# Two matmuls instead of three for the transposed products: both activation parts side by side as one 512-wide moving operand

## The chip, the cores and the metric

One NeuronCore of a Trainium2 chip. The metric is the device time of one execution in microseconds. The engines that matter here: PE (matrix multiply, with its weight load PEld), DVE (VectorE), ACT (ScalarE), SP (issues the DMAs). PE multiplies a stationary operand of 128x128 by a moving operand (here of 128 to 512 columns) and writes fp32 sums into PSUM, from which DVE and ACT read them. The program's PSUM pools hold eight banks of 512 fp32 columns: four for the products' sums, four for everything else.

## The reference

A stack of three layers on 256 tokens of 2048 features, all in fp32. What matters is that nearly all work is products of the activations with large weights:

```python
proj = jnp.einsum("bsd,de->bse", x, w_in) + b_in            # layer 1: conv branch, windowed attention
h = x @ w_in                                                 # layer 2: indexer-selected attention
q, g = _split(x @ w_q, (ATTN_W_2, ATTN_W_2))                 # layer 3: stick-breaking attention
x = _layer_norm(DN_ALPHA * x + y, ln_g[i], ln_b[i])          # after each
x = x + (p[i] @ w_ple[i]) * jax.nn.sigmoid(x @ w_ple_gate[i])
```

## The kernel before

Every product is made in a reduced-precision fp32 type (fp32r) from exact parts: an operand is rounded to a high part and the rest is its low part. A product is then three matmuls: high x high, high x low, low x high. Weights stream from DRAM in granules of 128 x 1024 (512 KB): a granule is loaded by SP (L247), rounded by ACT (`whi`, L265), and the rest is taken by DVE (`wlo`, L266). `whi` and `wlo` have four buffers each, and the code fetches two granules ahead of the one in use. The activations (`Act`) lie transposed, [feature, token], in tiles of four K tiles (K tile: 128 features), high and low parts in tiles of their own.

Two routines make the products, both a loop over the 16 K tiles of a chunk of weight columns. `gemm` has the activations stationary and up to 512 weight columns moving; it gives [token, column]. `gemm_T` has 128 weight columns stationary and 256 tokens moving; it gives [column, token], and makes three matmuls of 128x256 per K tile and 128 columns (L325 high x high, L326 high x low, L327 low weights x high). A chunk of `gemm_T` is 512 columns, in two PSUM tiles of one bank; the pool `acc` has four banks.

After a chunk its sums are read out of PSUM directly: by ACT with bias and function (`projected`, L468, in layer 1; `silu_chunk`, L964), by DVE and ACT in `glu` (L493), by DVE's rotation (`rope_T`, L839 and L840, for `Turned`), and by `Split` (L987 ACT high part, L988 DVE low part, L991 ACT copy). Between granules `side.pump()` hands out steps of other work (the convolution L481, attention, norms) to all engines. Each engine runs its instructions in the order that the tile scheduler fixed when the program was built.

Of the kernel before, what the change touches and what calls it, by code (L numbers as in the profile page):

```python
# [45 lines left out]
# Per weight: the chunks in the order of use, each as (column ranges, K tiles).  # L46
# [3 lines left out]
def _pairs(base, j):  # L50
    """Heads i and 8 + i side by side, for i of the j-th four."""
    return tuple(r for i in range(4 * j, 4 * j + 4) for r in ((base + 64 * i, 64), (base + 512 + 64 * i, 64)))
# [3 lines left out]
    **{f"vg{c}": ((CV + 256 * c, 256), (CG + 256 * c, 256)) for c in range(4)},  # L56
    "kv": _c(KK, 256),
    "q0": _pairs(QQ, 0),
    "ag0": _pairs(AG, 0),
    "q1": _pairs(QQ, 1),  # L60
    "ag1": _pairs(AG, 1),
    "cg0": _c(CT, 512),
    "cg1": _c(CT + 512, 512),
}
CHUNKS_1 = {key: (ranges, ALL) for key, ranges in CHUNKS_1.items()}
# The last columns of a row of the residual in smaller chunks.
# [10 lines left out]
    "k": (_c(2048, 512), ALL),  # L77
    "v": (_c(2560, 512), ALL),
    **{f"{n}{c}": (_c(o + 512 * c, 512), ALL) for c in range(4) for n, o in (("q", 0), ("g", 3072))},
# [3 lines left out]
CHUNKS_KV = {f"{n}{c}": (_c(o + 512 * c, 512), ALL) for c in range(4) for n, o in (("k", 0), ("v", 2048))}  # L83
CHUNKS_QB = {f"{n}{c}": (_c(o + 512 * c, 512), ALL) for c in range(4) for n, o in (("q", 0), ("g", 2048))}
# [15 lines left out]
def _plan():  # L100
    """The chunks in the order of their products."""
    w2 = [("w_in_a_2", key) for key in CHUNKS_2]
    w3 = [(w, f"{n}{c}") for c in range(4) for w, n in (("w_kv_b_2", "k"), ("w_q_b_2", "q"), ("w_kv_b_2", "v"), ("w_q_b_2", "g"))]
# [13 lines left out]
def _group(ranges, kts):  # L117
    """K tiles loaded at a time: about 4 KB a partition, less at the start."""
    if ranges == CHUNKS_1["vg0"][0]:
        return 1  # L120
# [3 lines left out]
def _column_tiles(chunks):  # L124
    """Per chunk, the number of its first tile of 128 columns."""
# [15 lines left out]
class Side:  # L141
    """Work beside the stream of weights, given out in small steps from each of some lanes."""
# [30 lines left out]
def tile_net(ctx: ExitStack, tc: tile.TileContext, t: dict, out: bass.AP):  # L173
# [10 lines left out]
    acc = ctx.enter_context(tc.tile_pool(name="acc", bufs=4, space=bass.MemoryType.PSUM))  # L184
# [29 lines left out]
    # additive mask [q, keys]: own block causal | previous block s > q, own block causal  # L214
# [25 lines left out]
    def load(stream, key, g):  # L240
        """The chunk's weights for a group of K tiles, on their way from DRAM."""
# [14 lines left out]
    def fetch(p, keep=False):  # L256
        """A group of weights as two exact parts."""
# [10 lines left out]
    def prefetch(*wanted):  # L268
        """The first groups of some chunks ahead of their turn, in steps."""
# [9 lines left out]
    def granules(stream, key, events):  # L279
        """The chunk's weights as they come: K tile, its first and last flags, both parts."""  # L280
# [35 lines left out]
    def gemm_T(stream, key, act, events=None):  # L316
        """[column, token] per two tiles of 128 columns."""
        nf = _cols(STREAMS[stream][key][0]) // P
        ps = [acc.tile([P, 2, S], F32, tag="acc", name=uid("acc")) for _ in range(nf // 2)]
        for kt, first, last, wh, wl in granules(stream, key, events):  # L320
            ah, al = act(kt, slice(0, S))
            for f in range(nf):
                o = ps[f // 2][:, f % 2, :]
                fs = slice(f * P, (f + 1) * P)
                nc.tensor.matmul(o, wh[:, fs], ah, start=first and f % 2 == 0, stop=False)  # L325
                nc.tensor.matmul(o, wh[:, fs], al, start=False, stop=False)  # L326
                nc.tensor.matmul(o, wl[:, fs], ah, start=False, stop=last and f % 2 == 1)  # L327
        return ps

    class Act:  # L330
        """Activations transposed, [feature, token], as two exact parts."""

        def __init__(self, kts=ALL):
            quarters = sorted({kt // 4 for kt in kts})
            self.hi = {q: unit((P, 4, S), F32R) for q in quarters}
            self.lo = {q: unit((P, 4, S), F32R) for q in quarters}

        def __call__(self, kt, s):
            q, k = divmod(kt, 4)
            return self.hi[q][:, k, s], self.lo[q][:, k, s]  # L340

        def parts(self, kt, n):
            q, k = divmod(kt, 4)
            return self.hi[q][:, k:k + n, :], self.lo[q][:, k:k + n, :]
# [6 lines left out]
    def transposes(blocks):  # L351
        """[token, 128] blocks -> a bank of them transposed, side by side."""
# [5 lines left out]
    def transpose_into(act, kt, nat, f0, n=2):  # L358
        """n K tiles from features f0.. of nat [token, token tile, feature]."""
# [4 lines left out]
    def turn_T(dst, nat, blocks):  # L364
        """128 features at a time of nat [token, token tile, feature] -> dst [feature, block, token]."""
# [31 lines left out]
    class Norm:  # L397
        """Layer norm over the features of z, [token, token tile, 512] per tile."""
# [9 lines left out]
        def apply(self, act):  # L408
            """z to (z - mean) / deviation in place; the operand of the products with scale and shift."""
# [23 lines left out]
        def affine(self):  # L433
            """Scale and shift of z itself, for the residual."""
# [6 lines left out]
    # ================= layer 1 =================  # L441
# [21 lines left out]
    def projected(key, out_, func, skip=0, events=None):  # L463
        """A chunk of the input projection, [column, token], with its bias and func."""
        ps = gemm_T("w_in", key, xact, events)
        for f in range(skip, 2 * len(ps)):
            b = tiles1[key] + f
            nc.scalar.activation(out_[:, f - skip, :], ps[f // 2][:, f % 2, :], func, bias=bias1[:, b:b + 1])  # L468
        return ps
# [14 lines left out]
    def glu(c):  # L484
        sg = short((P, 2, S))
        events = {kt: (lambda kt=kt: load_x(kt)) for kt in range(0, KT, 2)} if c == 0 else None
        if c == 0:
            load = events[14]
            events[14] = lambda: (load(), load_params())
        ps = projected(f"vg{c}", sg, AF.Sigmoid, 2, events)  # L490
        for f in range(2):
            ct, b = 2 * c + f, tiles1[f"vg{c}"] + f
            nc.vector.scalar_tensor_tensor(  # L493
                hT[ct // 4][:, ct % 4, :], ps[0][:, f, :], bias1[:, b:b + 1], sg[:, f, :], ALU.add, ALU.mult
            )
            side.add(conv(ct), CONV_RATE[ct % 2], "conv")
# [3 lines left out]
    def soften(heads, mask, scale):  # L500
        """Transposed probabilities [key, query] of some heads, in steps; the last value is a list."""
# [55 lines left out]
    def weigh(o, v, p):  # L557
        """o [feature, query] = values under the transposed probabilities of both blocks of keys."""
# [570 lines left out]
```

## Time and profile before

| | |
|---|---|
| three runs | 1467.13, 1467.75, 1468.92 us; median 1467.75 |
| the profiled execution | span from first to last instruction 1465.3 us |
| PE busy | 1453.9 us (99%), 10092 matmuls |
| PEld busy | 1353.8 us (92%) |
| DVE busy | 1000.1 us (68%) |
| ACT busy | 768.0 us (52%) |
| three lines of `gemm_T` | 6048 of the 10092 matmuls |

A group's row reads: line, engine, operation, out<-in by the program's names, shape, count | busy us, mean ns of one | idle time before it and what ended it. Matmuls are pipelined: the duration of one is longer than the distance from its start to the next one's, and the distance is what a stream of them costs.

### The profile page before, as it was taken

Reading aid. Unit: us, or ns where it says so; the run is one execution under the profiler, and the core shown is the slowest. Engines: PE = TensorE matmul, PEld = TensorE weight load, DVE = VectorE, ACT = ScalarE, POOL = GpSimd, SP = SyncE. Lnnn points to the kernel's source line nnn. Section 1 sums busy time; section 2 is a strip of 40 time slices with the busy share of each in tenths; the row PEclk is TensorE's granted clock in tenths of the full one; section 3 lists DMA queues with packets and bytes.
Section 4 is the critical chain, followed back from the end, with each engine's and each line's share of the span. In section 5 each row is a group of like instructions: output and inputs, shape, how many; then the busy total and the mean of one; then the engine's idle time right before and its main releaser. Section 6 shows DMA issues by size and latency. Waiting matters only on the chain.

```text
span 1465.3 us, 25141 instructions
## 1 busy us (share of the span) xinstructions
PE 1453.9 (99%) x10092; PEld 1353.8 (92%) x10092; DVE 1000.1 (68%) x1529; ACT 768.0 (52%) x1133; POOL 24.2 (2%) x51
## 2 busy tenths in 40 slices
PE   8999999999999999999999999999999999999998
PEld 8999999888997999999898899899999998989888
DVE  6998888898679857756758664545555556475854
ACT  6345777465544456546544444644655646554442
POOL 0000000000000000000000000100100001000000
PEclk9999999999999999999999999999999999999999
DMA  9855544556384655455765666555556565587472
GB/s 308 275 186 173 158 159 145 185 185 225 98 249 150 201 151 166 148 172 157 260 195 152 183 176 185 163 170 187 162 171 176 169 175 170 172 266 218 129 221 81
DMA packets 79813, 266.27 MB, mean 182 GB/s; under 512 B 9408, under 2 KB 10048, under 8 KB 79696
## 3 DMA queue, kind: packets, MB, share of 16 engines
q1 hardware_dynamic: 79632, 264.63, 58.8%
q8 instruction: 79, 1.29, 0.4%
q14 instruction: 38, 0.31, 0.1%
q0 software_dynamic: 64, 0.03, 0.0%
HBM read 262.53 MB, written 2.10 MB: 181 GB/s over the span
## 4 chain that ended last, share of the span: by engine, by line
PE 97%; DVE 1%; DMA 0%; issue 0%; ACT 0%; DVEq 0%
PE acc L325 17%; PE acc L326 16%; PE acc L327 16%; PE acc L311 14%; PE acc L312 14%; PE acc L313 14%; PE pt L355 1%; PE o L568 1%; PE pT L544 1%; PE o L569 0%; PE z L1024 0%; PE s L511 0%; PE z L1006 0%; PE o L559 0%; PE s L509 0%; PE z L1010 0%
## 5 line engine op out<-in xcount | busy, mean ns | idle before, releaser
L266 DVE TENSOR_TENSOR wlo<-raw,whi 128x1024 fp32r<-128x1024 f32 (+3 forms) x475 | 564.7, 1190 | 368.9 <-ACT whi L265 367.7
L265 ACT CAST whi<-raw 128x1024 fp32r<-128x1024 f32 (+3 forms) x475 | 485.4, 1024 | 551.7 <-PE acc L326 287.9
L325 PE MATMUL acc<-u,whi 128*128 128x256 f32 x2016 | 576.3, 286 | 5.5 <-ACT whi L265 5.5
L327 PE MATMUL acc<-u,wlo 128*128 128x256 f32 x2016 | 571.5, 283 | 0.0
L326 PE MATMUL acc<-u,whi 128*128 128x256 f32 x2016 | 571.3, 283 | 0.0
L325 PEld LDWEIGHTS acc<-u,whi 128*128 128x128 f32 x2016 | 387.6, 192 | 10.6 <-ACT whi L265 5.5
L326 PEld LDWEIGHTS acc<-u,whi 128*128 128x128 f32 x2016 | 387.8, 192 | 0.0
L327 PEld LDWEIGHTS acc<-u,wlo 128*128 128x128 f32 x2016 | 387.5, 192 | 0.0
L311 PE MATMUL acc<-whi,u 128*128 128x512 f32 (+3 forms) x1004 | 358.7, 357 | 0.0
L313 PE MATMUL acc<-whi,u 128*128 128x512 f32 (+3 forms) x1004 | 356.2, 355 | 0.0
L312 PE MATMUL acc<-wlo,u 128*128 128x512 f32 (+3 forms) x1004 | 355.6, 354 | 0.0
L313 PEld LDWEIGHTS acc<-whi,u 128*128 128x128 f32 x1004 | 189.8, 189 | 25.0 <-DVE u L349 0.2
L311 PEld LDWEIGHTS acc<-whi,u 128*128 128x128 f32 x1004 | 189.8, 189 | 24.8 <-issue 1.3
L312 PEld LDWEIGHTS acc<-wlo,u 128*128 128x128 f32 x1004 | 189.9, 189 | 23.6 <-issue 0.3
L481 DVE SCALAR_TENSOR_TENSOR u<-u,convw,u 128x255 f32<-128x255 f32 (+16 forms) x240 | 110.3, 466 | 4.5
L348 ACT CAST u<-h 128x512 fp32r<-128x512 f32 (+1 forms) x32 | 18.1, 567 | 31.8 <-DVE h L581 24.4
L349 DVE TENSOR_TENSOR u<-h,u 128x512 fp32r<-128x512 f32 (+1 forms) x32 | 19.9, 622 | 16.5 <-ACT u L348 16.5
L438 DVE TENSOR_TENSOR u<-u,h 128x1024 f32<-128x1024 f32 x24 | 28.4, 1220 | 3.3 <-DMA h<-in_ln_g 3.3
L996 POOL TENSOR_SCALAR_AFFINE_SELECT h<-h 128x256 f32<-128x256 f32 x32 | 18.1, 565 | 757.6 <-DVE h L1016 734.8
L524 ACT ACTIVATE u<-u,negm 128x128 f32<-128x128 f32 x64 | 28.4, 445 | 3.9 <-DVE negm L516 3.7
L265 ACT CAST u<-raw 128x1024 fp32r<-128x1024 f32 (+1 forms) x17 | 17.2, 1014 | 14.7 <-DMA raw<-in_w_ple 9.1
L426 ACT ACTIVATE h<-pt,normp 128x256 f32<-128x256 f32 x48 | 22.2, 618 | 0.0
(192 smaller groups left out, 932.0 us busy)
## 6 DMA issues: line engine op xcount, KB each, us to landing
raw<-in_w_in_a SPq DMA_DIRECT2D x80, 512.0 KB, 3.8
raw<-in_w_in SPq DMA_DIRECT2D x76, 512.0 KB, 3.6
raw<-in_w_gate SPq DMA_DIRECT2D x64, 512.0 KB, 4.0
raw<-in_w_kv_b SPq DMA_DIRECT2D x64, 512.0 KB, 3.6
raw<-in_w_q_b SPq DMA_DIRECT2D x64, 512.0 KB, 3.6
raw<-in_w_out SPq DMA_DIRECT2D x32, 512.0 KB, 3.6
raw<-in_w_out_a SPq DMA_DIRECT2D x32, 512.0 KB, 3.9
raw<-in_w_out_b SPq DMA_DIRECT2D x32, 512.0 KB, 4.4
```

Source lines behind the costliest of these rows:

```text
L265: nc.scalar.copy(hi, raw)
L266: return hi, lo, nc.vector.tensor_tensor(lo, raw, hi.bitcast(F32), ALU.subtract)
L311: nc.tensor.matmul(o, ah, wh, start=first, stop=False)
L312: nc.tensor.matmul(o, ah, wl, start=False, stop=False)
L313: nc.tensor.matmul(o, al, wh, start=False, stop=last)
L325: nc.tensor.matmul(o, wh[:, fs], ah, start=first and f % 2 == 0, stop=False)
L326: nc.tensor.matmul(o, wh[:, fs], al, start=False, stop=False)
L327: nc.tensor.matmul(o, wl[:, fs], ah, start=False, stop=last and f % 2 == 1)
L426: nc.scalar.activation(v[:, i, :], pt[:, i * S:(i + 1) * S], AF.Identity, bias=normp[:, self.i, 1, kt + i:kt + i + 1], scale=normp[:, self ...
L438: nc.vector.tensor_tensor(self.z[c], self.z[c], r.unsqueeze(1).broadcast_to([P, 2, 512]), op)
L481: nc.vector.scalar_tensor_tensor(o[:, d:], h[:, :S - d], w, o[:, d:], ALU.mult, ALU.add)
L524: nc.scalar.activation(sc[:, i, cs], sc[:, i, cs], AF.Exp, bias=negm[:, i, tt:tt + 1], scale=-1.0, accum_out=den[:, i, tt:tt + 1],)
```

## The change

`gemm_T` makes two matmuls per K tile and 128 columns. `Act` now holds, for each K tile, the high part and the low part next to each other (256 + 256 columns), and the first matmul has high weights against all 512 of these columns; its sums fill a whole bank, high x high in columns 0 to 255 and high x low in 256 to 511. The second has low weights against the high part and adds to columns 0 to 255. The two halves must be added afterwards: the new `total` copies the second half to SBUF with ACT (with bias or scale) and adds the first half with DVE. Since 128 weight columns now fill a bank, chunks of `gemm_T` are 256 columns (two banks) instead of 512 (two banks); `acc` has two tiles of two banks. `gemm` takes its two banks as one such tile. All readers of `gemm_T`'s sums go by `total`'s result. The first chunk of layer 1 stays at 512 columns. Comments and docstrings were dropped as well.

```diff
-    acc = ctx.enter_context(tc.tile_pool(name="acc", bufs=4, space=bass.MemoryType.PSUM))
+    acc = ctx.enter_context(tc.tile_pool(name="acc", bufs=2, space=bass.MemoryType.PSUM))
...
     def gemm(stream, key, act, events=None):
-        ps = [acc.tile([P, 512], F32, tag="acc", name=uid("acc")) for _ in range(2)]
+        both = acc.tile([P, 2, 512], F32, tag="acc", name=uid("acc"))
+        ps = [both[:, tt, :] for tt in range(2)]
...
     def gemm_T(stream, key, act, events=None):
         nf = _cols(STREAMS[stream][key][0]) // P
-        ps = [acc.tile([P, 2, S], F32, tag="acc", name=uid("acc")) for _ in range(nf // 2)]
+        ps = [acc.tile([P, 2, 2, S], F32, tag="acc", name=uid("acc")) for _ in range(nf // 2)]
         for kt, first, last, wh, wl in granules(stream, key, events):
-            ah, al = act(kt, slice(0, S))
+            both, ah = act.both(kt), act(kt, slice(0, S))[0]
             for f in range(nf):
-                o = ps[f // 2][:, f % 2, :]
+                o = ps[f // 2][:, f % 2]
                 fs = slice(f * P, (f + 1) * P)
-                nc.tensor.matmul(o, wh[:, fs], ah, start=first and f % 2 == 0, stop=False)
-                nc.tensor.matmul(o, wh[:, fs], al, start=False, stop=False)
-                nc.tensor.matmul(o, wl[:, fs], ah, start=False, stop=last and f % 2 == 1)
+                nc.tensor.matmul(o, wh[:, fs], both, start=first, stop=False)
+                nc.tensor.matmul(o[:, 0, :], wl[:, fs], ah, start=False, stop=last)
         return ps
 
+    def total(out_, ps, bias=None, scale=1.0):
+        t = short((P, 2, S))
+        if bias is None:
+            nc.scalar.activation(t, ps[:, :, 1, :], AF.Copy, scale=scale)
+        else:
+            for f in range(2):
+                nc.scalar.activation(t[:, f, :], ps[:, f, 1, :], AF.Identity, bias=bias1[:, bias + f:bias + f + 1])
+        out_ = t if out_ is None else out_
+        if scale == 1.0:
+            nc.vector.tensor_tensor(out_, ps[:, :, 0, :], t, ALU.add)
+        else:
+            nc.vector.scalar_tensor_tensor(out_, ps[:, :, 0, :], scale, t, ALU.mult, ALU.add)
+        return out_
+
     class Act:
         def __init__(self, kts=ALL):
-            quarters = sorted({kt // 4 for kt in kts})
-            self.hi = {q: unit((P, 4, S), F32R) for q in quarters}
-            self.lo = {q: unit((P, 4, S), F32R) for q in quarters}
+            self.pairs = {p: unit((P, 2, 2, S), F32R) for p in sorted({kt // 2 for kt in kts})}
+
+        def both(self, kt):
+            return self.pairs[kt // 2][:, kt % 2].rearrange("p h s -> p (h s)")
...
     def silu_chunk(stream, key, act):
-        ps = gemm_T(stream, key, act)
         sg = unit((P, 4, S))
-        for f in range(2):
-            nc.scalar.activation(sg[:, 2 * f:2 * f + 2, :], ps[f], AF.Silu)
+        for f, h in enumerate("xy"):
+            ps, = gemm_T(stream, f"{key}{h}", act)
+            nc.scalar.activation(sg[:, 2 * f:2 * f + 2, :], total(None, ps), AF.Silu)
...
     class Split:
...
-                nc.scalar.activation(self.hi[:, hs, :], p, AF.Copy, scale=scale)
-                nc.vector.scalar_tensor_tensor(
-                    self.lo[:, hs, :], p, scale, self.hi[:, hs, :].bitcast(F32), ALU.mult, ALU.subtract
-                )
-                nc.scalar.activation(self.late[:, hs, :], p[:, :, P:S], AF.Copy, scale=scale)
+                p, = gemm_T(stream, f"{name}{h}", xact)
+                w = total(None, p, scale=scale)
+                nc.scalar.copy(self.hi[:, hs, :], w)
+                nc.vector.tensor_tensor(self.lo[:, hs, :], w, self.hi[:, hs, :].bitcast(F32), ALU.subtract)
+                nc.scalar.copy(self.late[:, hs, :], w[:, :, P:S])
```

The first rows of PE's order, where layer 1's first chunk begins. `u_103` and `u_107` are the high and low parts of the first K tiles in the kernel before; in the changed one `u_103` holds both. Before:

```order
L325 MATMUL acc_131<-u_103,whi_139 128x256
L326 MATMUL acc_131<-u_107,whi_139 128x256
L325 MATMUL acc_132<-u_103,whi_139 128x256
L327 MATMUL acc_131<-u_103,wlo_140 128x256
L325 MATMUL acc_131<-u_103,whi_139 128x256
L326 MATMUL acc_131<-u_107,whi_139 128x256
L327 MATMUL acc_131<-u_103,wlo_140 128x256
L326 MATMUL acc_132<-u_107,whi_139 128x256
```

and in the changed kernel:

```order
L338 MATMUL acc_130<-u_103,whi_138 128x512
L339 MATMUL acc_130<-u_103,wlo_139 128x256
L338 MATMUL acc_130<-u_103,whi_138 128x512
L339 MATMUL acc_130<-u_103,wlo_139 128x256
L338 MATMUL acc_131<-u_103,whi_138 128x512
L339 MATMUL acc_131<-u_103,wlo_139 128x256
```

Three rows of 256 columns became one of 512 and one of 256, and the first row now needs both parts of the activations.

DVE's order in layer 1 at the end of a chunk of the gated values, among weight granules (`wlo`) and convolution steps. Before:

```order
L266 TENSOR_TENSOR wlo_806<-raw_769,whi_805 128x1024
L493 SCALAR_TENSOR_TENSOR u_116<-acc_477,bias_115,h_476 128x256 x2
L481 SCALAR_TENSOR_TENSOR u_118<-u_116,convw,u_118 128x232
L481 SCALAR_TENSOR_TENSOR u_118<-u_116,convw,u_118 128x254
L481 SCALAR_TENSOR_TENSOR u_118<-u_116,convw,u_118 128x231
```

and in the changed kernel:

```order
L278 TENSOR_TENSOR wlo_678<-raw_649,whi_677 128x1024
L510 SCALAR_TENSOR_TENSOR u_118<-u_116,convw,u_118 128x234
L352 TENSOR_TENSOR h_638<-acc_530,h_638 128x512
L510 SCALAR_TENSOR_TENSOR u_118<-u_116,convw,u_118 128x233
L529 TENSOR_TENSOR u_116<-h_638,h_525 128x512
L510 SCALAR_TENSOR_TENSOR u_118<-u_116,convw,u_118 128x232
L694 SCALAR_TENSOR_TENSOR u_670<-u_670,h_673 128x512
L510 SCALAR_TENSOR_TENSOR u_118<-u_116,convw,u_118 128x231
L694 SCALAR_TENSOR_TENSOR u_670<-u_670,h_673 128x512
```

The two 256-wide gates became one 512-wide sum (L352) and one 512-wide product (L529); the sigmoid's chunk has a sum of its own earlier.

ACT's order in layer 3 at the end of the first key chunk (`Split`). Before:

```order
L265 CAST whi_9993<-raw_9956 128x1024
L987 ACTIVATE u_9982<-acc_9740 128x512
L265 CAST whi_10023<-raw_9997 128x1024
L991 ACTIVATE h_9984<-acc_9740 128x256
L987 ACTIVATE u_9982<-acc_9741 128x512
L265 CAST whi_10053<-raw_10027 128x1024
L991 ACTIVATE h_9984<-acc_9741 128x256
```

and in the changed kernel:

```order
L277 CAST whi_8694<-raw_8676 128x1024
L346 ACTIVATE h_8665<-acc_8576 128x512
L277 CAST whi_8716<-raw_8698 128x1024
L1028 CAST u_8573<-h_8665 128x512
L1030 COPY h_8575<-h_8665 128x256
L277 CAST whi_8738<-raw_8720 128x1024
L277 CAST whi_8770<-raw_8742 128x1024
L277 CAST whi_8792<-raw_8774 128x1024
L346 ACTIVATE h_8760<-acc_8671 128x512
```

Of PSUM ACT now reads only the second half (L346); the high part and the copy come from SBUF, and the second 256 columns follow four granules later instead of at once.

## Rows read from the trace of the kernel before

**Rows 1.** The page: busy time of each engine with its share of the span, and DVE's busy tenths and the granted TensorE clock in 40 slices of the span.

```profile
PE 1453.9 (99%) x10092; PEld 1353.8 (92%) x10092; DVE 1000.1 (68%) x1529; ACT 768.0 (52%) x1133; POOL 24.2 (2%) x51
...
DVE  6998888898679857756758664545555556475854
...
PEclk9999999999999999999999999999999999999999
```

**Rows 2.** All waits of PE in the whole span: engine and line, what it waited for, us in total, times, longest.

```profile
PE acc L325 <- ACT whi L265: 5.5, 1, 5.5
PE ix L889 <- ACT h L892: 0.6, 1, 0.6
PE acc L311 <- DVE u L431: 0.2, 1, 0.2
```

**Rows 3.** Groups by shape: the three matmuls of `gemm_T`, one of their weight loads, and the 512-wide matmul of `gemm`.

```profile
L325 PE MATMUL acc<-u,whi 128*128 128x256 f32 x2016 | 576.3, 286 | 5.5 <-ACT whi L265 5.5
L327 PE MATMUL acc<-u,wlo 128*128 128x256 f32 x2016 | 571.5, 283 | 0.0
L326 PE MATMUL acc<-u,whi 128*128 128x256 f32 x2016 | 571.3, 283 | 0.0
...
L326 PEld LDWEIGHTS acc<-u,whi 128*128 128x128 f32 x2016 | 387.8, 192 | 0.0
...
L311 PE MATMUL acc<-whi,u 128*128 128x512 f32 x632 | 249.3, 395 | 0.0
```

**Rows 4.** Timeline of PE in a steady stretch of `gemm_T` (layer 2): start, duration, instruction. First and last of 70 rows that follow each other.

```profile
500.07 0.28 PE L325 MATMUL acc<-u,whi 128*128 128x256 f32 x1
...
508.35 0.28 PE L325 MATMUL acc<-u,whi 128*128 128x256 f32 x1
```

**Rows 5.** Timeline of PE in a steady stretch of `gemm` with 512 columns: first and last of 15 rows.

```profile
289.70 0.39 PE L313 MATMUL acc<-whi,u 128*128 128x512 f32 x1
...
292.88 0.39 PE L312 MATMUL acc<-wlo,u 128*128 128x512 f32 x1
```

**Rows 6.** Timeline of DVE, ACT and PE at the start of the program, and PE where its pace changes.

```profile
4.83 1.31 ACT L265 CAST whi<-raw 128x512 fp32r<-128x512 f32 x2
4.85 0.69 DVE L349 TENSOR_TENSOR u<-h,u 128x512 fp32r<-128x512 f32 x1 [3.74 <-ACT u L348]
...
5.51 0.58 PE L325 MATMUL acc<-u,whi 128*128 128x256 f32 x1 [5.51 <-ACT whi L265]
5.88 0.42 PE L326 MATMUL acc<-u,whi 128*128 128x256 f32 x1
6.10 0.42 PE L325 MATMUL acc<-u,whi 128*128 128x256 f32 x1
...
9.60 0.42 PE L325 MATMUL acc<-u,whi 128*128 128x256 f32 x1
9.81 0.41 PE L326 MATMUL acc<-u,whi 128*128 128x256 f32 x1
...
10.37 0.28 PE L326 MATMUL acc<-u,whi 128*128 128x256 f32 x1
10.49 0.28 PE L327 MATMUL acc<-u,wlo 128*128 128x256 f32 x1
```

**Rows 7.** Busy time of each engine in five stretches: layer 1's input projection (31 to 112 and 112 to 272 us), the index product of layer 2 (420 to 475), the rest of layer 2's input projection (475 to 683), and layer 3's projections (948 to 1268).

```profile
core 0: us, PE busy (x) PEld busy (x) DVE busy (x) ACT busy (x) POOL busy (x), PEclk, DMA share, GB/s
31.00:112.00 81.00, 81.00 (x678) 81.00 (x677) 78.84 (x138) 33.96 (x38) 0.00 (x0) 1.00 0.74 239
112.00:272.00 160.00, 159.95 (x1329) 152.50 (x1328) 136.83 (x289) 104.19 (x216) 0.20 (x1) 1.00 0.51 159
420.00:475.00 55.00, 54.42 (x357) 46.19 (x356) 50.08 (x104) 25.76 (x39) 1.81 (x2) 1.00 0.63 192
475.00:683.00 208.00, 208.00 (x1730) 207.00 (x1729) 142.52 (x272) 111.35 (x199) 0.00 (x0) 1.00 0.56 166
948.00:1268.00 320.00, 320.00 (x2388) 306.72 (x2388) 164.32 (x170) 172.11 (x232) 14.62 (x25) 1.00 0.57 172
```

**Rows 8.** Waits from 31 to 112 us, of all engines: the longest.

```profile
ACT whi L265 <- PE acc L326: 43.7, 26, 1.8
```

**Rows 9.** Groups by shape: the instructions that read `gemm_T`'s sums out of PSUM, an SBUF-only DVE instruction of 512 columns, and a function-table load.

```profile
L964 ACT ACTIVATE u<-acc 128x512 f32<-128x512 f32 x16 | 9.6, 597 | 0.4
L468 ACT ACTIVATE u<-acc,bias 128x256 f32<-128x256 f32 x24 | 9.8, 480 | 3.6 <-PE acc L327 3.6
L493 DVE SCALAR_TENSOR_TENSOR u<-acc,bias,h 128x256 f32<-128x256 f32 x8 | 3.5, 477 | 0.6 <-ACT h L468 0.6
L988 DVE SCALAR_TENSOR_TENSOR u<-acc,u 128x512 fp32r<-128x512 f32 x16 | 11.0, 687 | 4.8 <-ACT u L987 4.8
L841 DVE TENSOR_TENSOR h<-h,h 128x512 f32<-128x512 f32 x10 | 6.8, 684 | 0.0
L964 ACT ACT_TABLE_LOAD x8 | 10.3, 1283 | 0.1
```

**Rows 10.** Timeline of ACT and DVE in layer 3 from the end of a key or query chunk, its four reads of PSUM and the weight work between them.

```profile
996.50 0.60 ACT L987 ACTIVATE u<-acc 128x512 fp32r<-128x512 f32 x1 [1.23 <-PE acc L327]
...
997.10 1.05 ACT L265 CAST whi<-raw 128x1024 fp32r<-128x1024 f32 x1
997.12 0.69 DVE L988 SCALAR_TENSOR_TENSOR u<-acc,u 128x512 fp32r<-128x512 f32 x1 [0.60 <-ACT u L987]
...
998.17 1.23 DVE L266 TENSOR_TENSOR wlo<-raw,whi 128x1024 fp32r<-128x1024 f32 x1 [0.36 <-ACT whi L265]
...
1000.97 0.38 ACT L991 ACTIVATE h<-acc 128x256 f32<-128x256 f32 x1
```

More of the change, by code (lines that the diff above doesn't have):

```diff
@@ L50, in _pairs, with _twos @@
 def _pairs(base, j):
-    return tuple(r for i in range(4 * j, 4 * j + 4) for r in ((base + 64 * i, 64), (base + 512 + 64 * i, 64)))
+    return tuple(r for i in range(2 * j, 2 * j + 2) for r in ((base + 64 * i, 64), (base + 512 + 64 * i, 64)))
+def _twos(name, start):
+    return {f"{name}{h}": _c(start + 256 * i, 256) for i, h in enumerate("xy")}
 CHUNKS_1 = {
-    **{f"vg{c}": ((CV + 256 * c, 256), (CG + 256 * c, 256)) for c in range(4)},
+    "gv0": ((CG, 256), (CV, 256)),
+    **{f"{n}{c}": _c(o + 256 * c, 256) for c in range(1, 4) for n, o in (("g", CG), ("v", CV))},
     "kv": _c(KK, 256),
[L58 to L63, printed above, removed]
+    **{f"q0{h}": _pairs(QQ, i) for i, h in enumerate("xy")},
+    **{f"ag0{h}": _pairs(AG, i) for i, h in enumerate("xy")},
+    **{f"q1{h}": _pairs(QQ, 2 + i) for i, h in enumerate("xy")},
+    **{f"ag1{h}": _pairs(AG, 2 + i) for i, h in enumerate("xy")},
+    **_twos("cg0", CT),
+    **_twos("cg1", CT + 512),
 }
@@ L76 @@
     "i2": ((*_c(QI + 768, 256), (WI, 16), (KI, 64)), ALL),
-    "k": (_c(2048, 512), ALL),
+    **{key: (r, ALL) for key, r in _twos("k", 2048).items()},
     "v": (_c(2560, 512), ALL),
-    **{f"{n}{c}": (_c(o + 512 * c, 512), ALL) for c in range(4) for n, o in (("q", 0), ("g", 3072))},
+    **{key: (r, ALL) for c in range(4) for n, o in (("q", 0), ("g", 3072)) for key, r in _twos(f"{n}{c}", o + 512 * c).items()},
 }
@@ L82 @@
 CHUNKS_PLE = {f"{c}": (_c(512 * c, 512), (0, 1)) for c in range(4)}
-CHUNKS_KV = {f"{n}{c}": (_c(o + 512 * c, 512), ALL) for c in range(4) for n, o in (("k", 0), ("v", 2048))}
-CHUNKS_QB = {f"{n}{c}": (_c(o + 512 * c, 512), ALL) for c in range(4) for n, o in (("q", 0), ("g", 2048))}
+CHUNKS_KV = {
+    key: (r, ALL) for c in range(4)
+    for key, r in (*_twos(f"k{c}", 512 * c).items(), (f"v{c}", _c(2048 + 512 * c, 512)))
+}
+CHUNKS_QB = {
+    key: (r, ALL) for c in range(4) for n, o in (("q", 0), ("g", 2048)) for key, r in _twos(f"{n}{c}", o + 512 * c).items()
+}
 STREAMS = {
@@ L102, in _plan @@
     w2 = [("w_in_a_2", key) for key in CHUNKS_2]
-    w3 = [(w, f"{n}{c}") for c in range(4) for w, n in (("w_kv_b_2", "k"), ("w_q_b_2", "q"), ("w_kv_b_2", "v"), ("w_q_b_2", "g"))]
+    parts = (("w_kv_b_2", "k", "xy"), ("w_q_b_2", "q", "xy"), ("w_kv_b_2", "v", ("",)), ("w_q_b_2", "g", "xy"))
+    w3 = [(w, f"{n}{c}{h}") for c in range(4) for w, n, hs in parts for h in hs]
     square = lambda w: [(w, key) for key in CHUNKS_SQ]
@@ L117, in _group @@
 def _group(ranges, kts):
-    if ranges == CHUNKS_1["vg0"][0]:
+    if ranges == CHUNKS_1["gv0"][0]:
         return 1
@@ L340, in __call__ @@
-            return self.hi[q][:, k, s], self.lo[q][:, k, s]
+            u = self.pairs[kt // 2]
+            return u[:, kt % 2, 0, s], u[:, kt % 2, 1, s]
         def parts(self, kt, n):
-            q, k = divmod(kt, 4)
-            return self.hi[q][:, k:k + n, :], self.lo[q][:, k:k + n, :]
+            u = self.pairs[kt // 2]
+            ks = slice(kt % 2, kt % 2 + n)
+            return u[:, ks, 0, :], u[:, ks, 1, :]
         def put(self, kt, n, src):
@@ L461, in load_params, with projected @@
         nc.sync.dma_start(sink, bass.AP(tensor=t["sinks"].tensor, offset=t["sinks"].offset, ap=[[0, P], [1, 16]]))
[L463 to L469, printed above, removed]
+    def projected(key, out_, func=None):
+        ps, = gemm_T("w_in", key, xact)
+        if func is None:
+            total(out_, ps, tiles1[key])
+        else:
+            nc.scalar.activation(out_, total(None, ps, tiles1[key]), func)
     hT = [unit((P, 4, S)) for _ in range(2)]
@@ L927, in __init__ @@
             self.raw = short((P, 4, P))
-            for f, p in enumerate(ps):
+            for f, h in enumerate("xy"):
                 hs = slice(2 * f, 2 * f + 2)
+                p, = gemm_T("w_in_a_2", f"{name}{h}", xact)
                 w = short((P, 2, S))
-                rope_T(w, p)
+                rope_T(w, total(None, p))
                 nc.scalar.copy(self.hi[:, hs, :], w[:, :, tokens])
@@ L939, in head @@
             return SimpleNamespace(hi=self.hi[:, h, :], lo=self.lo[:, h, :], raw=self.raw[:, h, :])
-    kT2 = Turned(gemm_T("w_in_a_2", "k", xact), slice(0, S))
+    kT2 = Turned("k", slice(0, S))
     v2 = split_values(gemm("w_in_a_2", "v", xact))
@@ L968, in tile_net @@
     for c in range(4):
-        qT2 = Turned(gemm_T("w_in_a_2", f"q{c}", xact), slice(P, S))
+        qT2 = Turned(f"q{c}", slice(P, S))
         side.add(attn2(qT2, c, (0, 1), sgT), 1, "a")
@@ L1047, in tile_net @@
         for stream, name in (("w_kv_b_2", "k"), ("w_q_b_2", "q")):
-            ps = gemm_T(stream, f"{name}{c}", xact)
-            kq.append(Split(ps, SCALE2 if name == "q" else 1.0))
+            kq.append(Split(stream, f"{name}{c}", SCALE2 if name == "q" else 1.0))
         side.add(attn3(kq[1], kq[0], c, (0, 1), v3, sgT), 1, "a")
```

40 lines of the change are left out of this document (24 added, 16 removed).

## The prediction

> **What bounds the kernel now.** I read the page first, for the busy times: PE is busy for 99% of the span, DVE for 68%, ACT for 52%, and the granted clock is at its highest tenth in every slice [rows 1]. Since a busy PE may still be waiting in small pieces, I then asked for the waits of PE alone: it waited three times in 1465.3 us, 6.3 us in all, of which 5.5 us are the start of the program [rows 2]. So the time is the sum of what PE's own instructions take one after the other, and whatever shortens that stream shortens the kernel until another engine holds it up. Next the groups by shape, for the count: `gemm_T` issues 3 x 2016 matmuls of 256 columns [rows 3]. Their 283 ns are not what they cost, since they overlap. The cost is the distance from start to start, and the timeline has it: 8.28 us over 69 distances, 120.0 ns for 256 columns [rows 4]; 3.18 us over 14 distances, 227.1 ns for 512 columns in `gemm` [rows 5]. The weight load takes 192 ns [rows 3] and must therefore run beside earlier matmuls, since the matmuls start every 120 ns.
>
> **What is removed.** Doubling the columns adds 107.1 ns to 120.0, so a matmul costs 12.9 ns besides its columns. Three matmuls of 256 cost 360.0 ns; one of 512 and one of 256 cost 347.1. The columns are the same 768; what goes is one matmul's fixed part. Over 2016 triples that is 26.0 us. The timeline is printed to 10 ns, so 3.18 us may be wrong by 10 ns, or 0.7 ns a matmul: the term lies between 24.6 and 27.4 us. That a 512-wide matmul keeps its 227 ns when a 256-wide one with other weights follows is taken over from `gemm`, where weights also change at each matmul. At the start the spacing is 0.21 us for 256 columns until 10.2 us and 0.12 after [rows 6]; that is the lower of the two clock levels, and no fixed part shows there (0.21 us is 256 columns at 1.2 GHz). Those 22 matmuls are seven triples, so at most 0.1 us is lost from the term.
>
> **What is added on PE's path.** The first matmul now needs both parts of the activations. Before, it started at 5.51 us and the second, the first that needs the low part, at 5.88; DVE's low part ended at 4.85 + 0.69 = 5.54 [rows 6]. The first matmul will start up to 0.37 us later: 0.4 us at most, since a matmul's work was done in that time; I take 0.3.
>
> **What is added beside PE.** There are 2016 / 32 = 63 sets of 256 columns, and each gets one `total`. DVE: a sum of 512 columns out of PSUM, 687 ns by the nearest row [rows 9], 43.3 us in all. ACT: 597 ns for a copy of 512, or two of 480 with bias [rows 9]: 42 x 0.60 + 21 x 0.96 = 45.4 us, from which the removed biased reads (34 by the code, 34 x 0.48 = 16.3 us) go off; the sigmoids and SiLUs that remain run on 512 columns from SBUF, twelve at about 0.6. The built order has four more table loads, 1.3 us each [rows 9]. ACT goes from 768 to about 810 us and DVE from 1000 to about 1042 of a span of 1440: neither bounds the whole. What hides this work is PE's stream itself, as long as the weight parts, made on the same two engines, stay ahead of PE. If that cover were gone in full, the 43 us of DVE would stand in the time and the change would lose.
>
> So the stages decide. In layer 1 from 31 to 112 us DVE is busy for 78.84 of 81 us [rows 7], with the convolution between the weight granules. PE's 678 matmuls there are 7 sets. DVE gets 7 x 0.69 = 4.8 us more and loses 3 x (2 x 0.477 - 0.684) = 0.8 us at the gates [rows 9]: 82.8 us. PE needs 81 - 7 x 32 x 0.0129 = 78.1 us. DVE would fall 4.7 us behind. Whether PE feels it depends on the stock of finished weights. In this stretch ACT waited 26 times for PE to give back a `whi` buffer [rows 8], so the four buffers were full: one in use and three to come, 3 x 2.88 us, less the cast and subtraction of 1.05 and 1.23 us [rows 10], about 6.4 us of lead. The shortage of 4.7 us fits in. Price between 0 and 4.7; I take 0.4, since the lead early in the stretch is smaller than its end value. From 112 to 272 us there are 12 sets: DVE 136.83 + 8.2 = 145.0 us against PE's 160 - 5.0 = 155.0 [rows 7], free, and the stock refills. From 420 to 475 us DVE has 50.08 of 55 us; the first half of the key chunk's rotation now falls in there 11 us earlier than before (0.69 for the sum and about five DVE steps of 0.69), 54.2 us against 54.6 for PE: price 0 to 1.0, I take 0.2. From 475 to 683 and from 948 to 1268 DVE has over 65 and 155 us free [rows 7] for 16 and 24 sums, 11 and 16.5 us: nothing.
>
> **The sums' way out of PSUM.** With `acc` at two tiles of two banks, a set's banks are needed again when the next set ends, 16 x 2 x 347 ns = 11.1 us later; before, a 512-column chunk gave 23.0 us. In layer 3 the four reads of a chunk, with a cast and a subtraction between them, lasted from 996.50 to 1001.35 us, 4.9 us [rows 10]. `total` has two reads in a row (0.60 + 0.69) behind at most two granules in the built order, some 6 us. It fits in 11.1: nothing. `Split` and `Turned` even free their banks after two reads instead of three or four.
>
> **The sum.** -26.0 + 0.1 + 0.3 + 0.4 + 0.2 = -25.0 us. The profiled execution's span of 1465.3 becomes 1440.3. It lies 2.5 us under the median 1467.75, and I carry that over: **1442.8 us**, 1.7% less.
>
> **Rivals.**
> *DVE binds in layer 1.* For it: 97% busy already from 31 to 112 us. Against: the full buffers of [rows 8]. If the stock counts for nothing, the shortage of 4.7 us and 1.0 us in layer 2 stand in the time in place of 0.6: 1467.75 - 26.0 + 0.4 + 5.7 = 1447.9. Chance 0.10.
> *The fixed part doesn't go.* The change would not do what it says if the 12.9 ns went with the columns, or if a matmul of 512 next to one of 256 paid both. Then nothing is saved, and the time is 1467.75 + 0.9 = 1468.7 at worst, half of it at 1455. Against: the 512-wide rows have weights that change each time and pay 12.9 ns once. A stream with a smaller part per matmul, say a fifth of 12.9, would give 2016 x 2.6 ns = 5.2 us and 1463.4. The Trainium skill, page "TensorE: Matmul & The Clock Gate", section "Back-to-back issue gap", has such a rule: a full-clock gap of columns / 2.4 plus 2.5 ns; by it 2016 x 2.5 = 5.0 us would be won. The rows of this kernel show about five times that at both widths, and the measurement decides. Chance of this rival, all forms: 0.03.
> *The sums hold PE up (slower).* Place: the wait of a set's first matmul for its banks, 63 times. It decides from 25.0 / 63 = 0.40 us per set, that is when a set's two reads end later than 11.5 us after its last matmul. ACT and DVE run in order, so a `total` stuck behind attention or index work for 5 us more than reckoned would do it. Against: readers ended 4.9 us after the chunk even with more reads [rows 10]. With 1 us per set: 1442.8 + 63 = 1505. Chance 0.03.
>
> **How the numbers follow.** The forecast holds 0.84. Its own range is 24.6 to 27.4 us of gain with the additions between 0.1 and 1.5: 1440.4 to 1444.7. The range given reaches down to 1439.8 (the spread of the three runs) and up past the first rival to 1449.0. What this kernel's measurement can tell from no change is about 0.2%, 2.9 us. Faster: forecast, first rival and half of the second, 0.95; same 0.02; slower 0.03.
>
> **What would show it.** In the profile after: 2016 matmuls of 512 and 2016 of 256 columns, starts 227 + 120 ns apart (wrong: 240 + 120); PE's waits still some 6 us (if DVE binds: waits of PE on `wlo` between 40 and 115 us; if the sums bind: waits on ACT's or DVE's reads of `acc`); DVE near 98% from 30 to 110 us; PE's first matmul at 5.8 to 5.9 us. The prediction is wrong if a 512-wide matmul over the two parts costs more than 227 ns, or if PE waits for more than 10 us in all.

## The result, and the profile after

The changed kernel takes 1455.95 us (median of 4 runs, 1454.93 to 1456.16) against 1467.44 us for the kernel before: the ratio is 0.9921, with a 95% interval from 0.9907 to 0.9936. It is faster by 11.5 us. The forecast was 25 us, and 1455.95 lies above the top of its range, 1449.0. One execution of the experiments, the fourth of four and four, took 3923.73 us and counts as slow, so that version's median is of the other three.

The profiled execution took 1454.93 us, with a span of 1453.2 us. These lines of its page answer to [rows 1]:

```profile
PE 1437.5 (99%) x8076; PEld 1243.4 (86%) x8076; DVE 1033.6 (71%) x1588; ACT 803.4 (55%) x1199; POOL 24.3 (2%) x51
...
DVE  6999989998679966766758655555655555575754
...
PEclk9999999999999999999999999999999999999999
```

PE has 2016 matmuls less (10092 before), is busy for the same 99%, and its clock is as high as before. DVE and ACT gained 33.6 and 35.4 us, where some 42 us each were forecast. All waits of PE, which answer to [rows 2], and the two groups of `gemm_T` by shape, which answer to [rows 3]:

```profile
PE acc L338 <- DVE u L378: 5.7, 1, 5.7
PE acc L338 <- DVE h L352: 2.0, 1, 2.0
PE pt L384 <- DVE h L352: 1.2, 1, 1.2
PE acc L324 <- DVE u L460: 0.5, 2, 0.3
PE acc L325 <- DVE wlo L278: 0.5, 1, 0.5
PE pt L384 <- ACT h L455: 0.3, 1, 0.3
```

```profile
L338 PE MATMUL acc<-u,whi 128*128 128x512 f32 x2016 | 718.3, 400 | 7.7 <-DVE u L378 5.7 <-DVE h L352 2.0
L339 PE MATMUL acc<-u,wlo 128*128 128x256 f32 x2016 | 566.9, 281 | 0.0
```

The waits went from 6.3 to 10.2 us. Two are new: 2.0 us for the sums of the first chunk (`total`, line 352 of the changed kernel) and 1.2 us for those of `kv`, which the transposes behind that chunk need. Of the 3.9 us more, 0.9 were forecast (0.3, 0.4 and 0.2), so the waits explain 3.0 of the 13.5 us that are missing. Most of the rest is in the spacing. This is the timeline of PE in two stretches that hold only pairs of line 338 (512 wide) and 339 (256 wide). First and last of 97 rows from 480 us, then first and last of 191 rows from 40 us:

```profile
479.89 0.40 PE L338 MATMUL acc<-u,whi 128*128 128x512 f32 x1
...
496.85 0.40 PE L338 MATMUL acc<-u,whi 128*128 128x512 f32 x1
```

```profile
39.92 0.39 PE L338 MATMUL acc<-u,whi 128*128 128x512 f32 x1
...
72.85 0.39 PE L338 MATMUL acc<-u,whi 128*128 128x512 f32 x1
```

The first is 16.96 us over 48 pairs, 353.3 ns a pair. The second is 32.93 us over 95 pairs, 346.6 ns. The forecast was 347.1 everywhere. So the same pair of matmuls has two steady paces. By the starts of the whole trace, the short one runs 230 + 117 ns; the long one repeats three pairs, 241 + 120, 236 + 113 and 233 + 117. Of the 2016 pairs some 505 had the short pace (10 to 137 us, 154 to 163, 871 to 930, and two short stretches), and some 1500 the long one. Before the change every triple took 360.0 ns. Hence by this trace 505 x 13.3 + 1500 x 6.7 = 16.8 us were won by merging, where 26.0 were forecast.

### The profile page after: what moved, and what is told of

It is laid out like the page before. It is cut to its first block, busy times and chain, and to the rows that moved or that the text cites. A ratio compares the mean times of both kernels' runs of the same rounds, so it can differ in the third digit from the quotient of the medians.

```text
span 1453.2 us, 21296 instructions
## 1 busy us (share of the span) xinstructions
PE 1437.5 (99%) x8076; PEld 1243.4 (86%) x8076; DVE 1033.6 (71%) x1588; ACT 803.4 (55%) x1199; POOL 24.3 (2%) x51
## 4 chain that ended last, share of the span: by engine, by line
PE 90%; DVE 6%; DMA 2%; issue 1%; ACT 1%; DVEq 0%; SPq 0%; ACTq 0%
PE acc L338 28%; PE acc L339 14%; PE acc L324 14%; PE acc L326 14%; PE acc L325 14%; DVE wlo L278 2%; DVE u L510 2%; DMA raw<-in_w_in 1%; PE o L603 1%; PE pt L384 1%; PE pT L579 1%; PE o L604 0%; DVE u L449 0%; DMA h<-in_ln_b 0%; PE z L1063 0%
## 5 line engine op out<-in xcount | busy, mean ns | idle before, releaser
L338 PE MATMUL acc<-u,whi 128*128 128x512 f32 x2016 | 718.3, 400 | 7.7 <-DVE u L378 5.7
L338 PEld LDWEIGHTS acc<-u,whi 128*128 128x128 f32 x2016 | 379.4, 188 | 101.5 <-ACT whi L277 5.6
L339 PEld LDWEIGHTS acc<-u,wlo 128*128 128x128 f32 x2016 | 382.0, 189 | 0.3 <-DVE wlo L278 0.3
L510 DVE SCALAR_TENSOR_TENSOR u<-u,convw,u 128x255 f32<-128x255 f32 (+19 forms) x240 | 109.3, 466 | 3.9
L352 DVE TENSOR_TENSOR h<-acc,h 128x512 f32<-128x512 f32 x51 | 34.9, 685 | 5.5 <-ACT h L346 4.6
L377 ACT CAST u<-h 128x512 fp32r<-128x512 f32 (+1 forms) x32 | 18.0, 566 | 22.0 <-DVE h L616 15.6
L346 ACT ACTIVATE h<-acc 128x512 f32<-128x512 f32 x42 | 24.9, 594 | 5.1 <-PE acc L339 3.8
L803 DVE TENSOR_TENSOR h<-h,u 128x512 f32<-128x512 f32 (+1 forms) x20 | 10.8, 582 | 20.8 <-ACT h L802 20.8
```

Source lines behind the costliest of these rows:

```text
L338: nc.tensor.matmul(o, wh[:, fs], both, start=first, stop=False)
L339: nc.tensor.matmul(o[:, 0, :], wl[:, fs], ah, start=False, stop=last)
L346: nc.scalar.activation(t, ps[:, :, 1, :], AF.Copy, scale=scale)
L352: nc.vector.tensor_tensor(out_, ps[:, :, 0, :], t, ALU.add)
L510: nc.vector.scalar_tensor_tensor(o[:, d:], h[:, :S - d], w, o[:, d:], ALU.mult, ALU.add)
```

## The experiments

The question was why a 512-wide matmul does not keep its 226.7 ns beside a 256-wide one, and what the rest of the change costs. All edits are to the changed kernel unless said otherwise; they shift the line numbers of `gemm_T` and `total` in the rows by a few.

**Two wide, two narrow.** The order alone:

```diff
             for f in range(nf):
-                o = ps[f // 2][:, f % 2]
                 fs = slice(f * P, (f + 1) * P)
-                nc.tensor.matmul(o, wh[:, fs], both, start=first, stop=False)
-                nc.tensor.matmul(o[:, 0, :], wl[:, fs], ah, start=False, stop=last)
+                nc.tensor.matmul(ps[f // 2][:, f % 2], wh[:, fs], both, start=first, stop=False)
+            for f in range(nf):
+                fs = slice(f * P, (f + 1) * P)
+                nc.tensor.matmul(ps[f // 2][:, f % 2, 0, :], wl[:, fs], ah, start=False, stop=last)
```

> The order alone is changed: per K tile first the two 512-wide matmuls of a chunk's column tiles, then the two 256-wide ones (wide, wide, narrow, narrow instead of wide, narrow, wide, narrow); same work, same chunks. Theory A (in the changed kernel some 1500 of the 2016 pairs run at 353.3 ns, 505 at 346.7, and the strict alternation of a wide and a narrow matmul is what makes the slower pace possible): each pair costs 226.7 + 120.0 = 346.7 ns, 1500 x 6.7 = 10 us less than the changed kernel's 1456, so 1446 us (1444 to 1449). Theory B (the slower pace comes from the load on the other engines or from where weights and sums lie, and the order does not matter): 1456 us (1454 to 1458), with the two paces in the same places. Theory C (each change from wide to narrow costs something of its own): half of the changes go, so half of the 10 us: 1451.

It took 1451.05 us (ratio 0.9885, 0.9871 to 0.9900), 4.9 us less than the changed kernel. The order matters, so theory B falls. The time is theory C's (1451), and theory A's 346.7 ns is missed. Timeline of PE, first and last of 97 rows that each hold two matmuls:

```profile
40.12 0.63 PE L337 MATMUL acc<-u,whi 128*128 128x512 f32 x2
...
73.56 0.63 PE L337 MATMUL acc<-u,whi 128*128 128x512 f32 x2
```

33.44 us over 96 pairs is 348.3 ns, and the undisturbed pairs took 348.1 to 348.5 in every stretch of this trace: one pace, between the two. Here each turn from one width to the other also moves to the other bank, so the price is not that of writing again into the bank just written.

**Four wide, four narrow.** The loop of the experiment above over two K tiles at a time.

> The order alone is changed: over two K tiles first four 512-wide matmuls, then four 256-wide ones (at the first chunk and where the chunk has four column tiles, four and four of one K tile). Theory A: 346.7 ns a pair as with two and two, so the same 1446 us (1444 to 1449). Theory B: 1456. Theory C (a price on each change of width): a quarter of the changes is left, so 1456 - 0.75 x 10 = 1448.5, below the two-and-two order by 2.5.

It took 1453.72 us (0.9906, 0.9889 to 0.9922): more than half of the order's gain is gone. Neither A (1446) nor C (1448.5) is right. First and last of 47 rows of four matmuls:

```profile
40.32 1.09 PE L341 MATMUL acc<-u,whi 128*128 128x512 f32 x4
...
72.60 1.09 PE L341 MATMUL acc<-u,whi 128*128 128x512 f32 x4
```

32.28 us over 92 pairs is 350.9 ns. Fewer turns between the widths cost more in all, so a turn has no fixed price.

**Three matmuls of 256 in the new layout.** This takes back the merging alone:

```diff
+            al = act(kt, slice(0, S))[1]
...
-                nc.tensor.matmul(o, wh[:, fs], both, start=first, stop=False)
-                nc.tensor.matmul(o[:, 0, :], wl[:, fs], ah, start=False, stop=last)
+                nc.tensor.matmul(o[:, 0, :], wh[:, fs], ah, start=first, stop=False)
+                nc.tensor.matmul(o[:, 1, :], wh[:, fs], al, start=False, stop=False)
+                nc.tensor.matmul(o[:, 0, :], wl[:, fs], ah, start=False, stop=last)
```

> The changed kernel with its chunks of 256 columns, its layout and its sums, but three 256-wide matmuls for each set (high weights times the high part, high weights times the low part into the other half of the bank, low weights times the high part), as the kernel before had them. It prices all but the merging. Theory A (merging saves 1500 x 6.7 + 505 x 13.3 = 16.7 us, everything else costs about 4.5): 1467.4 + 4.5 = 1472 us (1470 to 1474). Rival D (the shortfall of 13 us is mostly the price of chunks and sums hidden in the stream, and merging saved the full 26 us): 1456 + 26 = 1482. Rival E (chunks and sums cost nothing): 1467.

It took 1472.25 us (1.0033, 1.0020 to 1.0045), as theory A said. So the chunks, the sums and the layout cost 4.8 us (2.9 to 6.6 by the interval), and merging brings 1472.25 - 1455.95 = 16.3 us. The steady spacing here is 120.0 ns for all three, as before. The operands' new places therefore don't cause the long pace. PE's waits show 2.5 + 0.8 = 3.3 us of the 4.8:

```profile
PE acc L339 <- ACT whi L277: 5.4, 1, 5.4
PE acc L339 <- DVE h L354: 2.5, 1, 2.5
PE pt L386 <- DVE h L354: 0.8, 1, 0.8
```

The profiled execution lost time behind these waits too. The longer one ended at 33.3 us, and these are the two stretches that follow (the number behind POOL's is the granted clock):

```profile
core 0: us, PE busy (x) PEld busy (x) DVE busy (x) ACT busy (x) POOL busy (x), PEclk, DMA share, GB/s
34.20:37.60 3.40, 3.40 (x18) 3.40 (x17) 2.58 (x5) 1.53 (x2) 0.00 (x0) 0.51 0.97 371
37.60:41.00 3.40, 3.40 (x30) 3.40 (x30) 2.89 (x5) 1.33 (x2) 0.00 (x0) 1.00 1.02 370
```

For 3.4 us the clock was at the lower of its two levels (1.2 GHz), 256 columns started 213 ns apart instead of 120, and about 1.5 us were lost. The traces of this series have five such falls between the start and the end of the program: here, at 115.6 us in two and two, at 33.6 and 122.3 us in the run with the zeros (next), and at 33.8 us in eight and eight. Each came within some 1.5 us of the end of a wait of 1.9 to 2.5 us for the sums of the first chunk or of `kv`. Three more such waits, of 1.8 to 2.5 us, had no fall behind them (in both traces of the changed kernel and in four and four), and no trace without such a wait has one. So a stall can cost more than its wait; that the wait brings the fall was not tested by itself. The tenths of PEclk on the page are too coarse to show it.

**A narrow matmul of zeros ahead of each group.** To see whether what runs ahead of a stretch picks its pace:

```diff
+            if not first and kt % 4 == 0:
+                nc.tensor.matmul(ps[0][:, 0, 1, 0:P], zero, ah[:, 0:P], start=False, stop=False)
```

> The changed kernel with one extra matmul of 128 columns (a block of zeros as weights, added to the sums, which changes nothing in them) at the start of each group of four K tiles but the first of a chunk, 186 in all, each 60 to 120 ns. Theory A2 (the pace is picked where the stream of pairs comes in after other matmuls and is kept until the next interruption; after 128-wide ones it was the fast pace in the changed kernel's trace): nearly all pairs behind such a matmul run at 346.7, 75% of the sets, so about 1100 slow sets become fast: -7.5 us + 186 x 0.07 to 0.12 (13 to 22 us) = 1462 to 1471 us, and the trace shows 346.7 throughout these groups. Rival B (load or placement decides): the paces stay where they were, 1469 to 1478, with some 1500 pairs at 353.3.

It took 1480.79 us (1.0092, 1.0077 to 1.0107), more than either theory said. The pairs behind it did not settle at the short pace: the mean of 1594 undisturbed pairs is 352.0 ns, and 136 of them took 346 or 347. Theory A2 falls. The extra matmul costs more than its own spacing, as its timeline shows:

```profile
60.34 0.22 PE L340 MATMUL acc<-u,zero 128*128 128x128 f32 x1
60.40 0.45 PE L344 MATMUL acc<-u,whi 128*128 128x512 f32 x1
60.68 0.28 PE L345 MATMUL acc<-u,wlo 128*128 128x256 f32 x1
```

The wide one follows 60 ns behind the zeros, but then needs 280 ns to the next start instead of 230 to 241: the short matmul moves part of its price to its neighbour. That it doesn't cover the next weight load (a record of 192 ns in [rows 3]) would explain it. It fits that the kernel before has 20 transposes of 128 columns, each with its own weight load, that start 109 ns apart (2.07 us over 19 distances from 365.95 us), but it wasn't tried by itself.

**Both matmuls 512 wide.** The decisive one: no mixture of widths is left in these products.

```diff
-                nc.tensor.matmul(o[:, 0, :], wl[:, fs], ah, start=False, stop=last)
+                nc.tensor.matmul(o, wl[:, fs], both, start=False, stop=last)
```

> The second matmul of each set is made 512 wide too (low weights times both parts, so low times low is added, which the reference's own rounding hides): only one width is left in these products. Theory A (mixing two widths costs the extra; one width alone has none): every wide matmul here starts 226.7 ns after the one before, as in the products that keep their weights as the moving operand; a set costs 453.3 ns, and the run is 1456 + 505 x (453.3 - 346.7) + 1500 x (453.3 - 353.3) = 1660 us. Rival F (a 512-wide matmul costs 233 ns in this orientation by itself, whatever its neighbour; in the order with two wide ones in a row they did start 233 apart): 466 a set, 1685 us.

It took 1661.41 us (one run), against 1660 by theory A and 1685 by rival F. Timeline of PE, first and last of 147 rows:

```profile
39.74 0.40 PE L339 MATMUL acc<-u,wlo 128*128 128x512 f32 x1
...
72.84 0.39 PE L339 MATMUL acc<-u,wlo 128*128 128x512 f32 x1
```

33.10 us over 146 distances is 226.7 ns. So the 512-wide matmul of this orientation is as cheap as the one in `gemm`, and it is the neighbours of another width that make it dearer.

**The changed kernel once more.**

> The changed kernel once more, for a second trace. If the pace of a stretch is fixed by the program (what stands before the stretch), the stretches at 346.7 ns lie in the same places as in the first trace: 10 to 137 us, 154 to 163 and 871 to 930, some 500 pairs in all. If it is chance, they lie elsewhere or their number differs by 100 or more.

It took 1455.54 us (one run). First and last of 189 rows in the stretch that had the short pace in the first trace:

```profile
39.75 0.40 PE L338 MATMUL acc<-u,whi 128*128 128x512 f32 x1
...
72.96 0.40 PE L338 MATMUL acc<-u,whi 128*128 128x512 f32 x1
```

33.21 us over 94 pairs is 353.3 ns. From 871 to 930 us it was the long pace too, and only some 130 pairs in all had the short one (mean of the undisturbed pairs 352.8 ns; 351.5 in the first trace). So the same program picks differently from run to run, though not everywhere: from 10 to 32 and from 116 to 136 us both traces had the short pace. What picks is open. Against the 360.0 ns of before, the two means give 2016 x 8.5 = 17.1 and 2016 x 7.2 = 14.5 us for merging, on either side of the 16.3 that the times gave.

**Without the two stalls.** The second half of the first chunk's sums goes to two banks of the other pool, and the transposes behind `kv` come one chunk later:

```diff
+        if nf == 4:
+            ps.append([bank("pv").rearrange("p (h s) -> p h s", h=2) for _ in range(2)])
...
-    pt = transposes([kvT[:, 1, tt * P:(tt + 1) * P] for tt in range(2)])
...
             projected(f"q{j}{h}", qT[j][:, 2 * f:2 * f + 2, :])
+            if j == f == 0:
+                pt = transposes([kvT[:, 1, tt * P:(tt + 1) * P] for tt in range(2)])
```

> The changed kernel's matmul order, with two stalls of the sums taken away: the second half of the first chunk's sums goes to two free banks of the other pool, so that the next chunk need not wait (2.2 us at 30 us), and the two transposes of the second layer-one value block are issued one chunk later (1.4 us at 113 us). Theory: the waits cost what they show, 1456 - 3.4 = 1452.5 us (1451 to 1454), less or more by up to 2 us if the pace of the pairs behind the two stalls changes with them: after both stalls the trace showed the fast pace, and without them 290 pairs may fall to the slow one (+1.9 us). Rival: the stalls were slack that comes back at a later wait: 1456.

It took 1453.44 us (0.9902, 0.9884 to 0.9919), 2.5 us under the changed kernel: inside the expected range, though the two intervals overlap, so this run alone shows little. All waits of PE that are left:

```profile
PE acc L340 <- DVE u L385: 5.6, 1, 5.6
PE acc L325 <- DVE wlo L278: 1.0, 1, 1.0
PE acc L324 <- DVE u L467: 0.5, 2, 0.3
PE pt L391 <- ACT h L462: 0.3, 1, 0.3
PE ix L935 <- ACT h L938: 0.3, 1, 0.3
```

Both stalls are gone. Nearly all pairs of this execution, the slowest of the four (1451.76 to 1455.45 us), had the long pace (mean 353.1 ns), and its span, 1453.8 us, was no shorter than that of the changed kernel. That is the trade which the expectation allowed for.

**Two wide, two narrow, without the stalls.**

> Both together: two wide, two narrow, and without the two stalls. If they add: 1451 - 3.4 = 1447.6 us (1446 to 1449). If the stalls are slack: 1451.

It took 1446.89 us (0.9861, 0.9846 to 0.9876), 4.2 us less than the order alone. The two gains come together: 9.1 us less than the changed kernel, where they were 4.9 and 2.5 by themselves. The trace of the order alone had a fall of the clock behind the stall at `kv` and this one has none, which may be why they bring more than their sum. This is the best version: 20.2 us under the kernel before, with an interval below that of the changed kernel. One wait is new, at 72.8 us in layer 1, and shows that the weight parts from DVE are close to holding PE up there:

```profile
PE acc L344 <- DVE wlo L278: 0.4, 1, 0.4
```

**Eight wide, eight narrow.** The four-and-four loop over four K tiles.

> The changed kernel's order alone: over four K tiles eight 512-wide matmuls, then eight 256-wide ones (the first chunk stays at four and four). Steady stretches so far: one and one 346.7 or 353.3 ns a pair, two and two 348.3, four and four 350.6, against 346.7 from two pure streams. Theory G (each turn of widths costs a fixed 15.6 ns at most, as in four and four, and dilutes): 346.7 + 15.6 / 8 = 348.6 a pair, 1454.3 - 2016 x 2.0 = 1450.3 us. Rival H (the wide ones stay near 234 as long as narrow ones are about, however few the turns): 350.6 or more, 1454 us or more, plus what later starts of a group's narrow weights cost.

It took 1452.60 us (0.9900, 0.9885 to 0.9915). First and last of 21 rows of eight matmuls:

```profile
42.33 2.00 PE L341 MATMUL acc<-u,whi 128*128 128x512 f32 x8
...
70.26 2.00 PE L341 MATMUL acc<-u,whi 128*128 128x512 f32 x8
```

27.93 us over 80 pairs is 349.1 ns, near theory G's 348.6 and off rival H's 350.6; the time lies between theirs (1450.3 and 1454). Against two and two the pace gives 0.8 ns x 2016 = 1.6 us more, and 1451.05 + 1.6 = 1452.7; 1452.60 was measured. This run shows where the price sits. The 16 distances of a cycle in ns, each the mean of 159 undisturbed cycles of the trace:

```
wide    233.2 235.8 228.3 232.4 230.8 226.7 226.7 226.6
narrow  113.4 119.1 120.0 120.0 120.0 120.0 120.0 120.0
```

Behind a turn to wide, five matmuls pay 27 ns together before the spacing is back at 226.7; behind a turn to narrow, two get 7.5 ns back. A full cycle costs 20 ns, that is 2.5 ns a pair here, and not theory G's 15.6. Shorter cycles are cut off before the spacing is back at 226.7, and pay 15 to 17 ns a cycle with four and four, 3.3 with two and two, and 6.7 or nothing with one and one. The table cut off after four of each gives 15.4, but after two of each 8.1, so the cutting off alone explains only the first. Why these sizes, and by which part of the engine, the runs don't show.

**The same mixture in the kernel before.** There the 512-wide products of `gemm`, whose spacing was 227.1 ns [rows 5], get it:

```diff
-                nc.tensor.matmul(o, ah, wl, start=False, stop=False)
+                for h in range(2 if n == 512 else 1):
+                    hs = slice(256 * h, 256 * h + 256) if n == 512 else slice(0, n)
+                    nc.tensor.matmul(o[:, hs], ah, wl[:, hs], start=False, stop=False)
```

> The kernel before the change, with the same mixture put where there was none: in the products that keep activations as weights, the middle one of each three 512-wide matmuls (low weights) is cut into two 256-wide ones, 688 times; the order there is wide, narrow, narrow, wide. One fixed part more each: 688 x 13.3 = 9.2 us. If mixing costs nothing in these products: 1467.4 + 9.2 = 1476.6 us, and the four start 226.7, 120.0, 120.0, 226.7 apart. If it costs as in the changed kernel's products with two and two (3.3 ns a turn): 1478.9, with wide starts of 230 to 236 in the trace; at 6.7 a turn: 1481.2.

It took 1476.87 us (1.0063, 1.0046 to 1.0080). The time cannot tell 1476.6 from 1478.9, but the timeline can: first and last line 311 of 19 cycles of wide, narrow, narrow, wide.

```profile
280.22 0.39 PE L311 MATMUL acc<-whi,u 128*128 128x512 f32 x1
...
293.46 0.40 PE L311 MATMUL acc<-whi,u 128*128 128x512 f32 x1
```

13.24 us over 19 is 696.8 ns, where the separate spacings give 693.4. It is 3.4 ns a cycle, as in `gemm_T` with two and two (2 x 348.3 = 696.6). The single distances are alike too: 233.2, 114.3, 116.5 and 233.0 ns here (577 undisturbed cycles), and in two and two 232.9, 233.3, 114.6 and 115.9. The price belongs to the widths, not to the product.

## Why the prediction was wrong, point by point

- **What bounds the kernel: right.** PE is busy for 99% before and after, and what shortens its stream shortens the kernel.
- **The term of 26.0 us: mis-sized, and this is the step that failed.** It took from `gemm` that "a 512-wide matmul keeps its 227 ns when a 256-wide one with other weights follows". The fixed part itself was right: 226.7 ns for wide ones alone and 120.0 for narrow ones alone. Mixed, the pair takes 346.7 or 353.3 ns, mostly the latter. The term measured 16.3 us. The prediction gave a width of 24.6 to 27.4 us for reading errors and none for this assumption, though no row of before had the two widths in one steady stream. Its second rival, "a matmul of 512 next to one of 256 paid both", named the place, but its chance was 0.03. Its half price is what the long pace costs, 6.7 of 13.3 ns. That the 1455 us it gave for half the price is also the time measured is in part luck: 3.8 us of the time are of another cause, below.
- **A smaller fixed part: no.** The streams of one width have 13.3 ns over the columns at 2.4 GHz (120.0 ns at 256, 226.7 at 512). The Trainium skill, page "TensorE: Matmul & The Clock Gate", section "Back-to-back issue gap", gives columns / 2.4 plus 2.5 ns at full clock for a matmul by itself; by that, as an estimate, 2016 x 2.5 = 5.0 us would be won. The trace does not agree, and 16.3 us were won.
- **The start: right.** The first matmul came 0.1 us later (at 5.65 us; 5.51 before [rows 6]; 0.3 was taken).
- **DVE in layer 1 and in the index product: right.** From 31 to 112 us DVE was busy for 79.36 of 81 us (78.84 before, [rows 7]), and PE never waited for `wlo` there. At 463 us it waited 0.5 us, within the bounds of 0 to 1.0.
- **"The sums' way out of PSUM ... fits in 11.1: nothing": wrong in one of 63 places.** The argument had a set's banks wanted again one set later. The first chunk has two sets that end together, so both tiles of the pool are full at once, and the next chunk waits 2.0 us. This is the third rival's mechanism, once instead of 63 times. The wait of the transposes behind `kv` for the same kind of sum, 1.2 us, was not reckoned at all. With it, and with the lower clock that stood behind such a wait in some executions, everything beside the merging costs 4.8 us where 1.0 was forecast.
- **The sum.** -16.3 + 4.8 = -11.5 us, against -26.0 + 1.0. Of the 13.5 us between, 9.7 are the mixed spacing and 3.8 the stalls and what else the new chunks and sums cost. Both signs that were to prove the prediction wrong came: the wide matmul costs more than 227 ns, and PE waits for 10.2 us.

## What to carry to other kernels

A price per instruction read in a stream of equal instructions holds for such a stream; where a change makes a mixture that no row shows, give the mixture its own bounds. Where two widths must alternate, try the order: two and two gained 4.9 us here for no work at all, while four and four lost more than half of it. When a chunk fills all the buffers of a pool at once, look at what follows it by itself, not at the average distance between uses. Behind a stall of PE, read the granted clock in a narrow window before its price is set equal to the wait.

## What the hardware showed unexpectedly

- An alternating stream of 512- and 256-wide matmuls has two steady paces, 346.7 and 353.3 ns a pair. Two executions of one program picked differently for the same stretch.
- After 256-wide matmuls the first five 512-wide ones take 228 to 236 ns instead of 226.7 (eight and eight). In the other orientation, with two in a row, they take 233.
- At the lower clock neither the fixed part nor the mixture has a price: in the falls above, the starts are 427 and 213 ns apart, which is 512 and 256 columns at 1.2 GHz.
- Behind five of eight waits of 1.8 to 2.5 us the clock was at 1.2 GHz for 3.4 us, at some 1.5 us each.
- A 128-wide matmul ahead of a group of these pairs cost 133 ns in all (24.8 us for 186), or 117 if the two falls of the clock in its trace (3.1 us) are taken off: some 60 by itself, and the rest at its neighbours.
